# PEER encoder trunk on one core: the second half of each layer without GpSimd splits, one-hot products or gate rows

## Chip, core and metric

One core of a Trainium2 chip runs the whole program in one launch. The metric is device time in microseconds (us), median of several runs. The engines are named as the profile names them: PE (TensorE matmuls), PEld (its weight loads), DVE (VectorE), ACT (ScalarE), POOL (GpSimd), SP (SyncE, which issues the DMAs).

## What is computed

A bidirectional encoder trunk with `DEPTH` 2, `SEQ` 256, `D_MODEL` 1024. Each layer is a mixer (five head groups between an input and an output projection) followed by a PEER feed-forward, and the change lies in the second:

```python
def peer_ffn(xn, wq, subkeys, u_tab, v_tab):
    q = (xn @ wq).reshape(b, s, PEER_HEADS, 2, PEER_HALF)              # 8 heads, 2 x 128
    sc = jnp.einsum('bshjc,hjkc->bshjk', q, subkeys)                   # 128 keys per half
    top_s, top_i = lax.top_k(sc, PEER_TOPK)                            # 16 of 128, twice
    cand = top_s[..., 0, :, None] + top_s[..., 1, None, :]             # 16 x 16 sums
    best, ci = lax.top_k(cand, PEER_TOPK)
    i1 = take(top_i[..., 0, :], ci // 16); i2 = take(top_i[..., 1, :], ci % 16)
    g = jax.nn.softmax(best)
    # per token: experts idx = i1 * 128 + i2, 8 x 16 of 16384
    act = gelu(u_tab[idx] . x);  y = sum((g * act) * v_tab[idx])
```

## The kernel before

The kernel does not gather experts. It multiplies all 16,384 rows of `u` with all 256 tokens, writes gelu of that into a table `H` of 128 partitions x (128 blocks x 256 tokens), multiplies `H` by a gate that is zero for experts a token did not choose, and multiplies the product with all of `v`.

**Weights.** Every weight comes as a block of 128 x 1024 fp32 numbers (`w_raw`) through `Stream` (lines 56 to 97). For precision each block is split into a rounded part and a rest: `w_hi` is a cast on ACT (L82), `w_lo` a subtraction (L84) on DVE, or on POOL where the block's flag in `sources` says so. The two parts have three buffers each (pool `hl`), so a block can be split when PE has finished the third block before it. Every product is three matmuls (L238 to L240: `w_hi` with `xh`, `w_hi` with `xl`, `w_lo` with `xh`). The flag comes from `queue(aps, pool_every)` (L144): from the fifth query block on every fourth block goes to POOL (L152 to L154).

**Order of the PEER phase** (`peer_phase`, L807 on). Eight pairs of query blocks (L969), then 64 pairs of `u` blocks (L974), then 128 `v` blocks (L981). A pair is 48 matmuls of 256 columns into `ps_mm`. Beside the pairs runs the routing of the tokens, in two tiles of 128 tokens, as a generator `routing_steps`: `score_steps` (scores, then 16 of 128 by max, index, replace, max, index: L808 to L812), `best_steps` (sums of candidates on POOL, L821; 16 of the 50 candidate pairs, L835 to L839; then the chosen pair's number as a one-hot row of 50 (L849), its product with the candidates' expert numbers on POOL (L851), and the sum over the row (L857)). Each `yield` names a cost, and after each half pair `bg.advance(budget)` lets the generator go on for `B_Q` or `B_R`. It must be done when `u` reaches block `U_FREE` (L976), since its tables lie in the second half of `H`.

**Gates.** After the routing each `u` pair is followed by one step `gate_step` for 8 tokens (32 steps): `a2`, a one-hot of `i2` (DVE, L892); `a1`, a one-hot of `i1` in bf16 (DVE, L895); `ag` = `a1` times the gate (POOL, L897); eight matmuls (L907) give each token's 128 x 128 gate; DVE multiplies it into the blocks of `H` that are done (L912), ACT copies it into the others (L911). Blocks that come later are multiplied on DVE as they are made (L932).

Program order is not the order on the engines: the framework's scheduler reorders by priority and its own model of durations. On each engine instructions then run strictly in the order that it wrote.

Of the kernel before, what the change touches and what calls it, by code (L numbers as in the profile page):

```python
# [12 lines left out]
BF16 = mybir.dt.bfloat16  # L13
# [3 lines left out]
ALU = mybir.AluOpType  # L17
# [3 lines left out]
P = 128  # L21
T = 256
D = 1024
NC = D // P
NK = 128
# [6 lines left out]
MEM_CHUNK = 2  # L32
FIRST = {0: 1, 1: 2}
B_Q = 1.3
B_R = 1.7
U_FREE = 64
W_IN_PAIRS = {"pool": 0, "conv_a": 2, "gate": 4, "diff_q": 6, "diff_k": 8, "diff_v": 10,
              "sc_h": 12, "sc_bg": 14, "sc_cg": 16, "mem_q": 18}
# [5 lines left out]
NPAIR = sum(PAIR_LEN)  # L44
# [92 lines left out]
def build(tc, x, mem, w_in, w_kv, w_out, wq, u_t, v_t, subk, pool_w, conv_pw, vec, dist, inv_count, ind, out, depth=2,  # L137
          dbg=None):
    nc = tc.nc
    V, A, G = nc.vector, nc.scalar, nc.gpsimd  # L140
# [3 lines left out]
    def queue(aps, pool_every=0):  # L144
        sources.extend((ap, pool_every > 0 and n % pool_every == pool_every - 1) for n, ap in enumerate(aps))

    for l in range(depth):
        queue([w_kv[l, b] for b in range(4)])
        queue([w_in[l, W_IN_PAIRS[n] + c] for n in MIX["pairs"] for c in range(2)], MIX["pool_every"])
        queue([w_out[l, 2 * g + c] for g in MIX["groups"] for c in range(2)], 3)  # L150
        queue([wq[l, b] for b in range(4)])
        queue([wq[l, b] for b in range(4, 16)], 4)  # L152
        queue([u_t[l, i] for i in range(NK)], 4)
        queue([v_t[l, i] for i in range(NK)], 4)  # L154

    with (
        tc.tile_pool(name="const", bufs=1) as cp,
# [16 lines left out]

        ind_t = cp.tile([P, 3, P], F32, name="ind_t")
        ones_m, ind64, ind32 = ind_t[:, 0, :], ind_t[:, 1, :], ind_t[:, 2, :]
        iota_t = cp.tile([P, NK, 8], BF16, name="iota_t")
        G.iota(iota_t, pattern=[[1, NK], [0, 8]], base=0, channel_multiplier=0, allow_small_or_imprecise_dtypes=True)
        iota_i = cp.tile([P, NK], BF16, name="iota_i")
        V.tensor_copy(iota_i, iota_t[:, :, 0])  # L180
        iota_f = cp.tile([P, NK], F32, name="iota_f")
        V.tensor_copy(iota_f, iota_t[:, :, 0])
        mhalf = cp.tile([P, 1], F32, name="mhalf")
        V.memset(mhalf, -0.5)
        warm = cp.tile([P, 1], F32, name="warm")
# [551 lines left out]
        def peer_phase(l, pp, pb):  # L737
# [8 lines left out]
            def pt(shape, name, bufs=1, dt=F32, tag=None):  # L746
                return pp.tile(shape, dt, name=name, bufs=bufs, tag=tag or name)
# [7 lines left out]
            def carve(n, dt=F32):  # L755
                nonlocal o
                s = hf[:, o:o + n]
                o += n
                assert o <= NK * T
                return s if dt is F32 else s.bitcast(dt)  # L760
# [5 lines left out]
            sk = carve(2048).rearrange("p (a k) -> p a k", a=16)  # L766
            nc.sync.dma_start(sk, subk[l])

            i1T = pt([P, T], "i1T", dt=BF16)
            i2T = pt([P, T], "i2T")  # L770
            gT = pt([P, T], "gT")

            work = [carve(128) for _ in range(2)]
            oh = [carve(8 * NPAIR, BF16).rearrange("p (k n) -> p k n", k=16) for _ in range(2)]
            pr = [carve(16 * NPAIR).rearrange("p (k n) -> p k n", k=16) for _ in range(2)]
            tabs = []
            for tt in range(2):
# [15 lines left out]
            def score_steps(tt):  # L793

                tb = tabs[tt]
                for hq in range(4):
                    while done["q"] < 2 * hq + 2:
                        yield None
                    ps = acc_tile(hq, [P, 4, NK], "ps_sc")
                    for r in range(4):  # L800
                        hj = 4 * hq + r
                        nc.tensor.matmul(ps[:, r, :], qT[:, hj // 2, hj % 2, tt * P:(tt + 1) * P], sk[:, hj, :],
                                         start=True, stop=True)
                    for r in range(4):
                        hj = 4 * hq + r
                        h, j = hj // 2, hj % 2
                        m0, m1 = tb["top_s"][:, h, j, 0:8], tb["top_s"][:, h, j, 8:16]  # L807
                        V.max(m0, ps[:, r, :])  # L808
                        V.max_index(tb["top_i"][:, h, j, 0:8], m0, ps[:, r, :])
                        V.match_replace(work[tt], m0, ps[:, r, :], -3e38)  # L810
                        V.max(m1, work[tt])
                        V.max_index(tb["top_i"][:, h, j, 8:16], m1, work[tt])  # L812
                        yield 1.8
                top_s, top_f = tb["top_s"], tb["top_f"]
                V.tensor_copy(top_f, tb["top_i"])
                V.tensor_scalar(top_f[:, :, 0, :], top_f[:, :, 0, :], 128.0, None, op0=ALU.mult)
                for dst, src in ((tb["cand"], top_s), (tb["ecand"], top_f)):
                    for a in range(9):
                        n, off = PAIR_LEN[a], PAIR_OFF[a]
                        if a < 8:  # L820
                            G.tensor_add(dst[:, :, off:off + n], src[:, :, 1, 0:n],  # L821
                                         src[:, :, 0, a:a + 1].to_broadcast([P, 8, n]))
                        else:
                            G.tensor_add(dst[:, :, off:off + 8], src[:, :, 0, 8:16],
                                         src[:, :, 1, 0:1].to_broadcast([P, 8, 8]))
                yield 0.6

            def best_steps(tt):

                tb = tabs[tt]  # L830
                best, bi, cand, ecand = tb["best"], tb["bi"], tb["cand"], tb["ecand"]
                wk = work[tt][:, :NPAIR]
                for h in range(8):
                    m0, m1 = best[:, h, 0:8], best[:, h, 8:16]
                    V.max(m0, cand[:, h, :])  # L835
                    V.max_index(bi[:, h, 0:8], m0, cand[:, h, :])
                    V.match_replace(wk, m0, cand[:, h, :], -3e38)
                    V.max(m1, wk)
                    V.max_index(bi[:, h, 8:16], m1, wk)  # L839
                    yield 1.3  # L840
                fin, gs = tb["fin"], tb["gs"]
                gx = fin[:, 2, :].rearrange("p (h k) -> p h k", h=8)
                V.tensor_sub(gx, best, best[:, :, 0:1].to_broadcast([P, 8, 16]))
                A.activation(gx, gx, AF.Exp)
                V.tensor_copy(tb["bib"], bi)
                yield 0.6

                def one_hot(h):
                    V.tensor_tensor(out=oh[h % 2], in0=iota_i[:, None, :NPAIR].to_broadcast([P, 16, NPAIR]),  # L849
                                    in1=tb["bib"][:, h, :, None].to_broadcast([P, 16, NPAIR]), op=ALU.is_equal)  # L850
                    G.tensor_mul(pr[h % 2], oh[h % 2], ecand[:, h, None, :].to_broadcast([P, 16, NPAIR]))  # L851

                one_hot(0)
                for h in range(8):
                    if h < 7:
                        one_hot(h + 1)
                    V.tensor_reduce(tb["es"][:, h, :], pr[h % 2], axis=AX.X, op=ALU.add)  # L857
                    yield 2.0
                ei = tb["ei"]
                V.tensor_copy(ei[:, 0, :], tb["es"].rearrange("p h k -> p (h k)"))  # L860
                V.tensor_scalar(ei[:, 1, :], ei[:, 0, :], 7, None, op0=ALU.arith_shift_right)
                V.tensor_scalar(ei[:, 2, :], ei[:, 0, :], 127, None, op0=ALU.bitwise_and)
                V.tensor_copy(fin[:, 0:2, :], ei[:, 1:3, :])
                yield 1.0
                V.tensor_reduce(gs, gx, axis=AX.X, op=ALU.add)
                V.reciprocal(gs, gs)
                V.tensor_mul(gx, gx, gs[:, :, None].to_broadcast([P, 8, 16]))
                yield 0.8
                ps = psum([P, 3, P], "ps_rt")
                for i in range(3):  # L870
                    nc.tensor.transpose(ps[:, i, :], fin[:, i, :], ident)
                s = slice(tt * P, (tt + 1) * P)
                A.copy(i1T[:, s], ps[:, 0, :])
                A.copy(i2T[:, s], ps[:, 1, :])
                A.copy(gT[:, s], ps[:, 2, :])
                yield 0.0
# [8 lines left out]
            GT = 8  # L885
            one_hots = {}

            def gate_one_hots(g):

                s = slice(GT * g, GT * g + GT)  # L890
                a2 = pt([P, GT, NK], "a2", bufs=2)
                V.tensor_tensor(out=a2, in0=iota_f[:, None, :].to_broadcast([P, GT, NK]),  # L892
                                in1=i2T[:, s, None].to_broadcast([P, GT, NK]), op=ALU.is_equal)
                a1 = pt([P, NK, GT], "a1", dt=BF16)
                V.tensor_tensor(out=a1, in0=iota_t, in1=i1T[:, None, s].to_broadcast([P, NK, GT]), op=ALU.is_equal)  # L895
                ag = pt([P, GT, NK], "ag", bufs=2)
                G.tensor_mul(ag, a1.rearrange("p i t -> p t i"), gT[:, s, None].to_broadcast([P, GT, NK]))  # L897
                one_hots[g] = (a2, ag)

            def gate_group(g):  # L900
# [176 lines left out]
```

## Time and profile before

| | |
|---|---|
| Median of 3 runs | 2061.68 us (2061.6 to 2062.93) |
| The profiled execution | 2062.52 us, of which its span 2060.7 us |
| PE busy | 1981.6 us (96%) |
| DVE busy | 1477.6 us (72%) |
| ACT, POOL busy | 984.4 us (48%), 769.5 us (37%) |
| `w_lo` on DVE, on POOL | 468 and 144 of them, mean 1.350 and 2.579 us |
| `ag` on POOL (L897) | 64, mean 3.016 us |
| Chain that ended last | PE 70%, DVE 21%, issue 3%, POOL 3% |
| DMA | 331.48 MB, mean 161 GB/s |

The two layers follow each other, 1021 us apart. In layer 0 the PEER phase's matmuls begin near 173 us, the routing lies between 188 and 384 us, the gates end near 666 us, and the `v` blocks run from 684 us to beyond 1030 us, into the next mixer. A share of the whole span says little here; each of these stretches has its own limit.

### The profile page before, as it was taken

To read this page: it belongs to the slowest core of one execution; us is meant where nothing else is said; L and a number is where in the kernel's file an instruction comes from. 1 tells how busy PE (TensorE), PEld (TensorE's weight loads), DVE (VectorE), ACT (ScalarE), POOL (GpSimd) and SP (SyncE) were. 2 spreads that over 40 slices of the span, in tenths; PEclk is the share of its full clock that TensorE was granted. 3 is DMA by queue.
4 is the path that set the end of the run, shared out by engine and by line. 5 is a ranking of instruction groups with operands and counts; after the bars stand their busy time and mean duration, and the time that the engine had idled before them with its cause. 6 is when DMAs were issued, how large, how long until landed. Compare 5 with 4: busy or idle time off the path is not lost.

```text
span 2060.7 us, 33441 instructions
## 1 busy us (share of the span) xinstructions
PE 1981.6 (96%) x13122; PEld 1818.7 (88%) x13122; DVE 1477.6 (72%) x2195; ACT 984.4 (48%) x1474; POOL 769.5 (37%) x430
## 2 busy tenths in 40 slices
PE   8899989899999999999999999889999999999999
PEld 7878988899999888888898789889999998888887
DVE  6875799669999554454478668995799995445454
ACT  7664444344433544444466644344444334444443
POOL 3721346435555222222236213572455541221221
PEclk9999999999999999999999999999999999999999
DMA  6324444444434655555553244435444345555554
GB/s 215 117 76 169 166 144 144 164 164 143 134 134 139 205 192 190 194 190 192 191 169 114 87 168 166 144 133 177 151 144 144 123 143 194 192 187 196 192 188 160
DMA packets 92766, 331.48 MB, mean 161 GB/s; under 512 B 10816, under 2 KB 11712, under 8 KB 92352
## 3 DMA queue, kind: packets, MB, share of 16 engines
q1 hardware_dynamic: 92608, 329.34, 47.0%
q8 instruction: 103, 1.69, 0.3%
q14 instruction: 55, 0.45, 0.1%
HBM read 328.25 MB, written 1.05 MB: 160 GB/s over the span
## 4 chain that ended last, share of the span: by engine, by line
PE 70%; DVE 21%; issue 3%; POOL 3%; ACT 2%; DMA 1%; SPq 0%; DVEq 0%; POOLq 0%; ACTq 0%
PE acc_v L268 11%; PE acc_v L271 11%; PE acc_v L267 11%; PE ps_mm L240 9%; PE ps_mm L238 9%; PE ps_mm L239 9%; DVE w_lo L84 6%; PE ps_g L907 4%; DVE H L849 2%; DVE H L857 1%; DVE a L892 1%; POOL cv_ac L436 1%; DVE H L932 1%; DVE a L895 1%; ACT w_hi L82 1%
## 5 line engine op out<-in xcount | busy, mean ns | idle before, releaser
L82 ACT CAST w_hi<-w_raw 128x1024 fp32r<-128x1024 f32 x612 | 641.4, 1049 | 790.1 <-PE ps_mm L239 445.5
L84 DVE TENSOR_TENSOR w_lo<-w_raw,w_hi 128x1024 fp32r<-128x1024 f32 x468 | 629.8, 1350 | 248.1 <-ACT w_hi L82 248.0
L240 PE MATMUL ps_mm<-xh,w_lo 128*128 128x256 f32 x2624 | 753.3, 288 | 39.0 <-DVE w_lo L84 36.8
L238 PE MATMUL ps_mm<-xh,w_hi 128*128 128x256 f32 x2624 | 754.5, 289 | 1.2 <-ACT H L934 1.2
L239 PE MATMUL ps_mm<-xl,w_hi 128*128 128x256 f32 x2624 | 749.5, 286 | 0.0
L84 POOL TENSOR_TENSOR w_lo<-w_raw,w_hi 128x1024 fp32r<-128x1024 f32 x144 | 371.3, 2579 | 892.4 <-ACT w_hi L82 872.5
L240 PEld LDWEIGHTS ps_mm<-xh,w_lo 128*128 128x128 f32 x2624 | 508.1, 194 | 46.2 <-DVE w_lo L84 43.4
L238 PEld LDWEIGHTS ps_mm<-xh,w_hi 128*128 128x128 f32 x2624 | 507.2, 194 | 3.1 <-ACT H L934 1.6
L239 PEld LDWEIGHTS ps_mm<-xl,w_hi 128*128 128x128 f32 x2624 | 508.7, 194 | 0.9 <-DVE xl L229 0.5
L268 PE MATMUL acc_v<-w_lo,a_hi 128*128 128x512 f32 x1016 | 316.5, 392 | 0.0
L271 PE MATMUL acc_v<-w_hi,a_lo 128*128 128x512 f32 x1016 | 315.4, 392 | 0.0
L947 DVE TENSOR_TENSOR a_lo<-H,a_hi 128x512 fp32r<-128x512 f32 x128 | 120.4, 942 | 239.1 <-ACT a_hi L945 239.0
L267 PE MATMUL acc_v<-w_hi,a_hi 128*128 128x512 f32 x1016 | 274.0, 391 | 0.0
L897 POOL TENSOR_TENSOR ag<-a,gT 128x1024 f32<-128x1024 bf16 x64 | 193.0, 3016 | 183.6 <-PE ps_g L907 104.1
L271 PEld LDWEIGHTS acc_v<-w_hi,a_lo 128*128 128x128 f32 x1016 | 190.9, 188 | 42.3
L267 PEld LDWEIGHTS acc_v<-w_hi,a_hi 128*128 128x128 f32 x1016 | 190.9, 188 | 41.6
L268 PEld LDWEIGHTS acc_v<-w_lo,a_hi 128*128 128x128 f32 x1016 | 191.1, 188 | 40.6
L945 ACT CAST a_hi<-H 128x512 fp32r<-128x512 f32 x128 | 79.4, 622 | 154.8 <-PE acc_v L268 149.6
L932 DVE TENSOR_TENSOR H<-tmp,H 128x16 f32<-128x16 f32 (+16 forms) x68 | 152.0, 2236 | 0.0
L907 PE MATMUL ps_g<-ag,a 128*128 128x128 f32 x1024 | 126.0, 275 | 1.3 <-POOL ag L897 1.3
L907 PEld LDWEIGHTS ps_g<-ag,a 128*128 128x128 f32 x1024 | 120.5, 192 | 1.7 <-POOL ag L897 1.7
L892 DVE TENSOR_TENSOR a<-iota_f,i2T 128x1024 f32<-128x1024 f32 x64 | 85.4, 1337 | 6.7 <-PE ps_g L907 6.7
(244 smaller groups left out, 1607.1 us busy)
## 6 DMA issues: line engine op xcount, KB each, us to landing
w_raw<-u_t SPq DMA_DIRECT2D x256, 512.0 KB, 3.3
w_raw<-v_t SPq DMA_DIRECT2D x256, 512.0 KB, 4.2
w_raw<-w_in SPq DMA_DIRECT2D x40, 512.0 KB, 3.5
w_raw<-wq SPq DMA_DIRECT2D x32, 512.0 KB, 3.3
w_raw<-w_out SPq DMA_DIRECT2D x20, 512.0 KB, 3.2
w_raw<-w_kv SPq DMA_DIRECT2D x8, 512.0 KB, 4.3
H<-subk SPq DMA_DIRECT2D x2, 1024.0 KB, 4.8
mem_t<-mem SPq DMA_DIRECT2D x4, 256.0 KB, 6.4
```

The lines of the kernel that those rows point to most:

```text
L82: self.nc.scalar.copy(hi, r)
L84: (self.nc.gpsimd if on_pool else self.nc.vector).tensor_sub(lo, r, hi.bitcast(F32))
L238: nc.tensor.matmul(ps, wh, xh[:, c, :], start=(c == 0), stop=False)
L239: nc.tensor.matmul(ps, wh, xl[:, c, :], start=False, stop=False)
L240: nc.tensor.matmul(ps, wl, xh[:, c, :], start=False, stop=(c == NC - 1))
L267: nc.tensor.matmul(accs[tt][hf], ah[:, s], hi[:, n], start=start, stop=False)
L268: nc.tensor.matmul(accs[tt][hf], ah[:, s], lo[:, n], start=False, stop=False)
L271: nc.tensor.matmul(accs[tt][hf], al[:, s], hi[:, n], start=False, stop=False)
L897: G.tensor_mul(ag, a1.rearrange("p i t -> p t i"), gT[:, s, None].to_broadcast([P, GT, NK]))
L907: nc.tensor.matmul(ps[:, t, :], a2[:, 4 * q + t, :], ag[:, 4 * q + t, :], start=True, stop=True)
L932: V.tensor_mul(sl[:, :, :g], tmp[:, :, :g], sl[:, :, :g])
L947: V.tensor_sub(al, src, ah.bitcast(F32))
```

## The change

From the query weights on no block is flagged for POOL, so DVE splits them all. The product L851 moves from POOL to DVE, and its one-hot row is laid out with the 16 chosen ranks innermost, compared against a table `iota_i` of 50 x 16. `a1` and its table `iota_t` go away: `ag` is made by eight DVE instructions of 128 elements, one for each token, that compare with `i1` and multiply by the gate at once, both given per partition; `i1T` is fp32 for that. POOL keeps the sums of candidates (L821, L824) there. `B_R` and the costs in the yields are others, so the generator is cut differently. The mixer's flags stay.

```diff
-B_R = 1.7
+B_R = 1.4
...
-        queue([wq[l, b] for b in range(4)])
-        queue([wq[l, b] for b in range(4, 16)], 4)
-        queue([u_t[l, i] for i in range(NK)], 4)
-        queue([v_t[l, i] for i in range(NK)], 4)
+        queue([wq[l, b] for b in range(16)])
+        queue([u_t[l, i] for i in range(NK)])
+        queue([v_t[l, i] for i in range(NK)])
...
-        iota_t = cp.tile([P, NK, 8], BF16, name="iota_t")
-        G.iota(iota_t, pattern=[[1, NK], [0, 8]], base=0, channel_multiplier=0, allow_small_or_imprecise_dtypes=True)
-        iota_i = cp.tile([P, NK], BF16, name="iota_i")
-        V.tensor_copy(iota_i, iota_t[:, :, 0])
+        iota_i = cp.tile([P, NPAIR, 16], BF16, name="iota_i")
+        G.iota(iota_i, pattern=[[1, NPAIR], [0, 16]], base=0, channel_multiplier=0, allow_small_or_imprecise_dtypes=True)
         iota_f = cp.tile([P, NK], F32, name="iota_f")
-        V.tensor_copy(iota_f, iota_t[:, :, 0])
+        G.iota(iota_f, pattern=[[1, NK]], base=0, channel_multiplier=0, allow_small_or_imprecise_dtypes=True)
...
-            i1T = pt([P, T], "i1T", dt=BF16)
+            i1T = pt([P, T], "i1T")
...
-            oh = [carve(8 * NPAIR, BF16).rearrange("p (k n) -> p k n", k=16) for _ in range(2)]
+            oh = [carve(8 * NPAIR, BF16).rearrange("p (n k) -> p n k", k=16) for _ in range(2)]
...
-                        yield 1.8
+                        yield 1.2
...
-                    yield 1.3
+                    yield 0.8
...
                 def one_hot(h):
-                    V.tensor_tensor(out=oh[h % 2], in0=iota_i[:, None, :NPAIR].to_broadcast([P, 16, NPAIR]),
-                                    in1=tb["bib"][:, h, :, None].to_broadcast([P, 16, NPAIR]), op=ALU.is_equal)
-                    G.tensor_mul(pr[h % 2], oh[h % 2], ecand[:, h, None, :].to_broadcast([P, 16, NPAIR]))
-
-                one_hot(0)
+                    V.tensor_tensor(out=oh[h % 2], in0=iota_i, in1=tb["bib"][:, h, None, :].to_broadcast([P, NPAIR, 16]),
+                                    op=ALU.is_equal)
+                    V.tensor_mul(pr[h % 2], oh[h % 2].rearrange("p n k -> p k n"),
+                                 ecand[:, h, None, :].to_broadcast([P, 16, NPAIR]))
+
                 for h in range(8):
-                    if h < 7:
-                        one_hot(h + 1)
+                    one_hot(h)
                     V.tensor_reduce(tb["es"][:, h, :], pr[h % 2], axis=AX.X, op=ALU.add)
-                    yield 2.0
+                    yield 2.4
...
-                a1 = pt([P, NK, GT], "a1", dt=BF16)
-                V.tensor_tensor(out=a1, in0=iota_t, in1=i1T[:, None, s].to_broadcast([P, NK, GT]), op=ALU.is_equal)
                 ag = pt([P, GT, NK], "ag", bufs=2)
-                G.tensor_mul(ag, a1.rearrange("p i t -> p t i"), gT[:, s, None].to_broadcast([P, GT, NK]))
+                for t in range(GT):
+                    k = GT * g + t
+                    V.tensor_scalar(ag[:, t, :], iota_f, i1T[:, k:k + 1], gT[:, k:k + 1], op0=ALU.is_equal, op1=ALU.mult)
```

Three places show how the order on the engines moves. Line numbers of the changed kernel are three lower through the routing and four lower from L857 on; `H<-H` is routing work, whose tables lie in `H`.

DVE, two gate steps of layer 0 before the change:

```order
L932 TENSOR_TENSOR H<-tmp,H 128x2x24
L892 TENSOR_TENSOR a_5034<-iota_f,i2T 128x1024
L912 TENSOR_TENSOR H<-ps_g,H 128x66x4 x2
L895 TENSOR_TENSOR a_5121<-iota_t,i1T 128x1024
L84 TENSOR_TENSOR w_lo<-w_raw,w_hi 128x1024 x2
L932 TENSOR_TENSOR H<-tmp,H 128x2x32
L892 TENSOR_TENSOR a_5119<-iota_f,i2T 128x1024
L912 TENSOR_TENSOR H<-ps_g,H 128x68x4 x2
L895 TENSOR_TENSOR a_5206<-iota_t,i1T 128x1024
L84 TENSOR_TENSOR w_lo<-w_raw,w_hi 128x1024
```

The same engine and place in the changed kernel:

```order
L928 TENSOR_TENSOR H<-tmp,H 128x2x24
L888 TENSOR_TENSOR a_4995<-iota_f,i2T 128x1024
L908 TENSOR_TENSOR H<-ps_g,H 128x64x4
L893 TENSOR_SCALAR ag<-iota_f,i1T,gT 128x128 x5
L908 TENSOR_TENSOR H<-ps_g,H 128x64x4
L893 TENSOR_SCALAR ag<-iota_f,i1T,gT 128x128 x3
L84 TENSOR_TENSOR w_lo<-w_raw,w_hi 128x1024 x2
```

A step now has two splits always, and eight short instructions in place of the compare L895.

DVE, one-hot rows of the first token tile in the changed kernel (a compare L846, a product L848, a sum L853 for each head):

```order
L84 TENSOR_TENSOR w_lo<-w_raw,w_hi 128x1024
L853 TENSOR_REDUCE H<-H 128x16
L846 TENSOR_TENSOR H<-iota_i,H 128x800
L853 TENSOR_REDUCE H<-H 128x16
L846 TENSOR_TENSOR H<-iota_i,H 128x800
L808 MAX H<-H 128x8
L84 TENSOR_TENSOR w_lo<-w_raw,w_hi 128x1024
L848 TENSOR_TENSOR H<-H 128x800
L84 TENSOR_TENSOR w_lo<-w_raw,w_hi 128x1024
L848 TENSOR_TENSOR H<-H 128x800
```

Before, L851 stood in POOL's order and DVE had L849 and L857 alone; heads now come in twos, with three splits between one pair of sums and the next.

POOL, from the last sums of candidates of layer 0 on, before the change:

```order
L824 TENSOR_TENSOR H<-H 128x8x8
L84 TENSOR_TENSOR w_lo<-w_raw,w_hi 128x1024
L897 TENSOR_TENSOR ag<-a_4690,gT 128x1024
L84 TENSOR_TENSOR w_lo<-w_raw,w_hi 128x1024
L897 TENSOR_TENSOR ag<-a_4696,gT 128x1024
L851 TENSOR_TENSOR H<-H 128x800 x4
```

and in the changed kernel:

```order
L818 TENSOR_TENSOR H<-H 128x8x2 x3
L821 TENSOR_TENSOR H<-H 128x8x8
L195 MEMSET mm_kz 128x1024
L195 MEMSET mm_vz 128x1024
L195 MEMSET pw 128x256
```

After the sums POOL has nothing until the next layer's mixer.

## Rows read from the trace of the kernel before

**Rows 1.** Stretches: us, busy (count) of PE PEld DVE ACT POOL, clock, DMA

```profile
260.00:400.00 140.00, 123.96 (x987) 121.49 (x986) 127.23 (x264) 55.82 (x67) 77.89 (x47) 0.96 0.43 147
600.00:690.00 90.00, 86.55 (x699) 84.58 (x698) 80.98 (x73) 37.84 (x71) 42.15 (x14) 1.00 0.45 153
720.00:1000.00 280.00, 280.00 (x1225) 229.94 (x1224) 139.45 (x127) 133.90 (x154) 62.73 (x26) 1.00 0.57 191
1281.00:1421.00 140.00, 123.74 (x985) 121.00 (x984) 127.27 (x262) 55.63 (x67) 78.25 (x47) 0.98 0.43 147
```

**Rows 2.** What PE waited for, whole span: us in total, times, longest

```profile
PE ps_mm L240 <- DVE w_lo L84: 36.8, 30, 3.2
```

**Rows 3.** PE in order of time, one gate step: start us, us, instruction

```profile
501.51 1.95 PE L907 MATMUL ps_g<-ag,a 128*128 128x128 f32 x16
...
503.41 0.28 PE L239 MATMUL ps_mm<-xl,w_hi 128*128 128x256 f32 x1
...
509.05 1.95 PE L907 MATMUL ps_g<-ag,a 128*128 128x128 f32 x16
510.75 0.36 PE L238 MATMUL ps_mm<-xh,w_hi 128*128 128x256 f32 x1
```

**Rows 4.** The first stretch, `ps_mm` matmuls alone: PE busy (count), clock

```profile
260.00:400.00 140.00, 119.33 (x934) 0.96 0.43 147
```

**Rows 5.** The gate step on DVE, then POOL, in order of time

```profile
500.60 0.68 DVE L895 TENSOR_TENSOR a<-iota_t,i1T 128x1024 bf16<-128x1024 bf16 x1
...
503.85 2.49 DVE L932 TENSOR_TENSOR H<-tmp,H 128x160 f32<-128x160 f32 x1
...
507.80 0.48 DVE L912 TENSOR_TENSOR H<-ps_g,H 128x320 f32<-128x320 f32 x1
...
503.54 2.63 POOL L897 TENSOR_TENSOR ag<-a,gT 128x1024 f32<-128x1024 bf16 x1 [4.94 <-PE ps_g L907]
507.37 2.76 POOL L84 TENSOR_TENSOR w_lo<-w_raw,w_hi 128x1024 fp32r<-128x1024 f32 x1 [1.21 <-ACT w_hi L82]
```

**Rows 6.** DVE by line and form, L932: busy us, mean ns, idle before

```profile
L932 DVE TENSOR_TENSOR H<-tmp,H 128x272 f32<-128x272 f32 x2 | 5.2, 2618 | 0.0
...
L932 DVE TENSOR_TENSOR H<-tmp,H 128x288 f32<-128x288 f32 x2 | 0.9, 446 | 0.0
...
L932 DVE TENSOR_TENSOR H<-tmp,H 128x16 f32<-128x16 f32 x2 | 0.3, 162 | 0.0
```

**Rows 7.** DVE in order of time, routing stretch

```profile
226.44 0.29 DVE L808 MAX8 H<-ps_sc 128x8 f32<-128x128 f32 x1
...
227.37 1.21 DVE L84 TENSOR_TENSOR w_lo<-w_raw,w_hi 128x1024 fp32r<-128x1024 f32 x1
228.49 0.09 DVE L810 MATCH_VALUE_LOAD H<-H,ps_sc 128x8 f32 x1
...
228.76 0.29 DVE L808 MAX8 H<-ps_sc 128x8 f32<-128x128 f32 x1
...
229.89 0.28 DVE L810 MATCH_REPLACE8 H<-H,ps_sc 128x128 f32<-128x128 f32 x1
230.20 0.30 DVE L811 MAX8 H<-H 128x8 f32<-128x128 f32 x1
...
247.23 0.87 DVE L835 MAX8 H<-H 128x8 f32<-128x50 f32 x7
...
283.55 0.96 DVE L857 TENSOR_REDUCE H<-H 128x16 f32<-128x800 f32 x1
284.44 0.97 DVE L849 TENSOR_TENSOR H<-iota_i,H 128x800 bf16<-128x800 bf16 x1
```

**Rows 8.** DVE with a scalar per partition: count, ns min/median/max, starts, form

```profile
L215 DVE TENSOR_SCALAR rn_ms<-rn_ss x8: 203/207/215, 16.8 to 1191.2; 128x1 f32<-128x1 f32 x8
...
L218 DVE TENSOR_SCALAR H<-xt,rn_rs x4: 475/482/486, 169.3 to 1192.1; 128x512 f32<-128x512 f32 x4
```

**Rows 9.** A DVE copy that reads bf16 at steps of 16 bytes, same columns

```profile
L180 DVE COPY iota_i<-iota_t x1: 261/261/261, 3.4 to 3.4; 128x128 bf16<-128x128 bf16 x1
```

## The prediction

> **What bounds the kernel now.** I read the busy time by stretches first, then PE's waits, then single instructions in order of time. Over the whole span PE looks full, so a gain can only come from stretches where it is not. In the `v` blocks it has no hole: 280.00 of 280 us [rows 1]. In 260 to 400 us, where the tokens are routed, it has 123.96 of 140, while DVE has 127.23; near the end of the gates (600 to 690) it has 86.55 of 90. Layer 1 repeats this 1021 us later. So 16.0 and 3.45 us a layer are PE's idle time. The waits name who ended it: PE's matmuls with `w_lo` waited 36.8 us for DVE's splits [rows 2], nearly all of twice 19.5. This is the whole field for the change, with what the clock adds.
>
> That part is found by counting matmuls. Between 503.41 and 509.05 lie 47 starts of `ps_mm`, 0.120 us each; the 16 passes of a gate burst take 1.70, 0.106 each; a whole gate step, 501.51 to 509.05, takes 7.54 [rows 3]. In 260 to 400 us PE did 934 `ps_mm` [rows 4] and 53 others: 934 x 0.120 + 53 x 0.106 = 117.7 us. It lost 22.3 of 140: 16.0 idle, 6.3 at the lower granted clock (mean 0.96 there) and in restarting. A layer thus loses 22.3 + 3.45 = 25.75 us, both 51.5.
>
> DVE's busy time is partly waiting. L932 on 160 elements took 2.49 us, and ended 0.17 after POOL's `ag`, which ran from 503.54 to 506.17; L912, which reads one side from PSUM, took 0.48 inside a POOL split [rows 5]. By form it is plainer: 288 elements took 0.446 us where POOL was free, 272 took 2.618 where it was not [rows 6]. A DVE instruction with two SBUF inputs waits here for POOL's to end.
>
> **The change, part by part.** Durations overlap: a split of 1.21 is followed 1.12 later by the next instruction [rows 7]. I use start to start, 0.08 less than a duration. From 16 and 288 elements [rows 6], an fp32 instruction costs 0.145 + 1.04 ns an element.
>
> *Gate steps.* Gone are the compare L895 and the POOL product with the waits that it caused. Added are half a split and eight `ag` instructions. One scalar per partition and one element take 0.207, 512 elements 0.482 [rows 8]: 0.54 ns an element, so 128 take 0.276, 0.195 start to start. No row has two scalars. If the second costs as much as the first (0.207 against 0.145), it is 0.255; at 1.04 ns an element it would be 0.32. Ends 0.195 and 0.32; I take 0.23, between the first two, since the rows with 512 elements are the nearest. The last step, the dearest: two splits 2.26, `a2` (a split's form) 1.13, eight `ag` 1.84, L912 twice on 4 x 120 and L932 on 2 x 240 elements, 1.69: 6.92 us under PE's 7.54. At 0.32 it is 7.64, which passes PE only in the last steps. So the 3.45 us go, twice: **6.9 us**.
>
> *Routing stretch.* The changed order on DVE is dense from the phase's 21st to its 64th weight block. Between those splits it holds: 44 splits, 49.7 us; 91 score instructions at 0.205 to 0.275 (five take 1.20, 226.44 to 228.76 less the split [rows 7]), 22.3; 80 on 50 elements (seven take 0.87 [rows 7], 0.115 each, 0.175 to 0.185 with a value load), 12.4; 16 products at 0.90, as the old compare of 800 elements (0.97), 14.4; 15 sums at 0.89, 13.4; 16 compares, whose inputs now both run contiguously in bf16 as L895's do, which took 0.68 for 1024 [rows 5], so 0.48, 7.7; four `a2` and 32 `ag`, 11.9; small ones 3.8. Sum 135.6 us. PE's own time for these blocks: 44 x 24 x 0.120 = 126.7, and 6.8 for scores, transposes and the two first gate groups: 133.5. So DVE is just over PE. To it come waits for its own results: L811 starts 0.31 after L810 where it needs it, 0.20 where something stands between [rows 7], so 0.11 each; bounds none and all 91 + 80, 19 us; I take 40 of them, 4.5, because the scheduler mixes two chains. From it goes a lead of about 3 (two blocks of 2.88, less cast and split). 135.6 + 4.5 - 133.5 - 3 = 3.6. The order is uneven: the first gate rows put 7.3 us between two splits, and the four blocks of the first one-hot heads hold 15.5 where PE needs 11.5. I add 2.5 for these two: 6 us idle, and 2 at the lower clock, by the ratio of today (6.3 to 16.0). Eight of 22.3 stay, 14.3 go, twice: **28.6 us**. Ends: 2 stay (no own waits, no clock), 40.6 won; 17 stay (most own waits exposed), 10.6 won.
>
> The product is the one new form in it, since it reads the one-hot row at steps of 32 bytes. A copy of 128 bf16 elements at steps of 16 bytes took 0.261 [rows 9], 0.91 ns an element over 0.145, no slower than an fp32 element; hence 0.90. The Trainium skill (SBUF — State Buffer, section on the DMA port swizzle, note on cachelines) says that SBUF has 16-byte lines and that an access to a new line each time pays a penalty, without an amount. This row shows none at 16 bytes; at 32 none is shown. By that rule the sum would be the first rival's.
>
> *At nothing.* In the `v` blocks DVE takes the fourth split, 1.13 in 11 us, of which it is busy half (139.45 of 280); the cover is that half, and without it a split would delay PE by its 1.13. The candidates' sums stay on POOL, and a DVE cast may still wait for one; that lies inside the ends above. Tables at the start are made while the first weights load. Mixer order is unchanged up to the query weights. No DMA changes; a raw buffer is freed by DVE in 1.2 us [rows 7] instead of by POOL in 2.8 [rows 5].
>
> **Sum.** The profiled execution took 2062.52 us (span 2060.7, 1.8 around it); the median of the runs is 0.84 lower. 2062.5 - 6.9 - 28.6 = 2027.0; against the median I say **2026 us**.
>
> **The rivals.**
> 1. *The product's stride costs.* At half as much or double per element, 16 products add 6.6 to 13.3 us a layer to a stretch where DVE is just over PE; with the clock's share 8 to 16. Time 2042 to 2058. For it: no row reads at 32 bytes. Against: the copy at 16. Chance 0.10.
> 2. *DVE stays the bound of the routing.* Own waits are hardly covered, since the new order has long runs of one chain (compare, product, sum of the same head), and 17 to 22 of 22.3 stay. Time 2045 to 2055. For it: DVE's sum is already level with PE's. Against: its waits behind POOL are gone. Chance 0.12.
> 3. *Slower: gate rows bound DVE.* A step is 4.08 + 0.033 j + 8 a, with a the start to start of one `ag` and j from 0 to 29. It passes 7.54 at the last step from a = 0.31 on. It eats the 17.75 us won in a layer when the sum of the excess over 30 steps reaches that: 0.1 x 30 + 14.5 at a = 0.445; from there the change loses. At 0.50 the excess is 30.7, 13 more than won, twice: 2088 us. For it: 256 instructions a layer of a form that no row has. Against: the rows with one scalar, which are half that. Chance 0.06.
> 4. *The wait was not POOL's.* If L932 keeps its 2.2 us without POOL, a gate step is 1 us over PE: 2 x (32 - 14.3) = 35 us slower, 2097. Against it stand both forms in one kernel [rows 6]. Chance 0.02.
>
> **How the numbers follow.** The forecast has 0.70, with its own range 2015 to 2045 from the ends above (2062.5 - 6.9 - 40.6 and - 10.6). The whole field is 51.5 us, so nothing lies under 2010. The range goes to 2012 at the low end, for a lead that I made too small, and to 2050 at the other, over most of rivals 1 and 2; outside stay rivals 3 and 4 and the tails, under 0.2. A measurement here tells about 0.2% from no change, 4.1 us, so faster means under 2057.6: 0.70 + 0.10 + 0.12 less their upper tails, 0.88. Same: 0.04. Slower: 0.08.
>
> **What would show it.** POOL has no split and no `ag` from the query weights on. L932's forms lie on one line, 0.16 to 0.69 us, with no step of 2.2. PE has no idle time in 600 to 690, and less than half of 16 in the routing. `ag` takes 0.27 to 0.34 us, the new compare near 0.56, the product near 0.97. I am wrong if PE still waits over 12 us a layer for `w_lo`, if the product takes 1.4 or more, or if DVE is full through the gate steps.

## The result and the profile after

The changed kernel took **2036.33 us** (median of 4 runs, 2035.27 to 2037.62) against 2062.01 of the kernel before: ratio 0.9875, 95% interval 0.9858 to 0.9892. The forecast was 2026, its range 2012 to 2050. So 26 us were won where 35.5 were forecast. The profiled execution spans 2033.5 us, 27.2 less than before.

The stretches of [rows 1] (first to third lines: routing, end of the gates, `v` blocks; fourth: the routing of layer 1):

```profile
260.00:400.00 140.00, 131.90 (x1062) 129.19 (x1061) 132.68 (x298) 60.91 (x73) 6.38 (x18) 0.99 0.47 158
600.00:690.00 90.00, 90.00 (x678) 86.31 (x678) 69.08 (x111) 42.37 (x73) 0.00 (x0) 1.00 0.51 171
720.00:1000.00 280.00, 280.00 (x1225) 229.94 (x1224) 160.38 (x153) 133.79 (x154) 0.00 (x0) 1.00 0.55 191
1281.00:1421.00 140.00, 130.07 (x1052) 126.75 (x1051) 124.09 (x245) 57.72 (x69) 6.37 (x18) 1.00 0.47 162
```

PE's idle time at the end of the gates is gone. In the routing it fell from 16.0 to 8.1 us in layer 0 and from 16.3 to 9.9 in layer 1. POOL is nearly empty. PE's wait for the splits, to be laid beside [rows 2]:

```profile
PE ps_mm L237 <- DVE w_lo L84: 16.5, 19, 1.5
```

Where the gain lies is read from two landmarks in each layer: the start of the second norm (L218 before [rows 8], L215 now) and the start of the last `ps_mm` matmul. First these matmuls before the change, layer 0, then layer 1 (count, ns, starts):

```profile
L240 PE MATMUL ps_mm<-xh,w_lo x1312: 275/283/583, 28.7 to 683.3; 128*128 128x256 f32 x188
L240 PE MATMUL ps_mm<-xh,w_lo x1312: 277/283/470, 1051.0 to 1704.3; 128*128 128x256 f32 x188
L218 DVE TENSOR_SCALAR H<-xt,rn_rs x2: 479/482/486, 169.3 to 171.5; 128x512 f32<-128x512 f32 x2
L218 DVE TENSOR_SCALAR H<-xt,rn_rs x2: 475/480/486, 1189.9 to 1192.1; 128x512 f32<-128x512 f32 x2
```

The same rows of the changed kernel:

```profile
L237 PE MATMUL ps_mm<-xh,w_lo x1312: 278/283/469, 29.3 to 669.2; 128*128 128x256 f32 x188
L237 PE MATMUL ps_mm<-xh,w_lo x1312: 278/283/470, 1036.9 to 1677.0; 128*128 128x256 f32 x188
L215 DVE TENSOR_SCALAR H<-xt,rn_rs x2: 476/481/486, 169.7 to 171.9; 128x512 f32<-128x512 f32 x2
L215 DVE TENSOR_SCALAR H<-xt,rn_rs x2: 478/482/485, 1175.7 to 1177.9; 128x512 f32<-128x512 f32 x2
```

From landmark to landmark: 514.0 and 514.4 us before, 499.5 and 501.3 now. That is 14.5 + 13.1 = 27.6 us, the whole difference of the spans (27.2) and 0.4 more; the mixer and the `v` blocks together gave nothing. Less the 3.45 us of the gates, the routing gave 11.0 and 9.7 us a layer where 14.3 were forecast.

The instructions that the change touches, on DVE (count, ns min/median/max, starts, form): the product, the compare, `ag`; then L928 (L932 before) by form, with busy us and mean ns, to be laid beside [rows 6]:

```profile
L848 DVE TENSOR_TENSOR H<-H x32: 1649/1694/1746, 270.6 to 1389.3; 128x800 f32<-128x800 bf16 x32
L846 DVE TENSOR_TENSOR H<-iota_i,H x32: 551/562/582, 267.9 to 1381.8; 128x800 bf16<-128x800 bf16 x32
L893 DVE TENSOR_SCALAR ag<-iota_f,i1T,gT x512: 325/342/394, 354.1 to 1644.1; 128x128 f32<-128x128 f32 x171
...
L928 DVE TENSOR_TENSOR H<-tmp,H 128x288 f32<-128x288 f32 x2 | 0.9, 452 | 0.0
L928 DVE TENSOR_TENSOR H<-tmp,H 128x272 f32<-128x272 f32 x2 | 0.9, 435 | 0.0
...
L928 DVE TENSOR_TENSOR H<-tmp,H 128x16 f32<-128x16 f32 x2 | 0.3, 170 | 0.0
```

272 elements, which took 2618 ns before, take 435. The compare is as forecast (0.56), `ag` at the upper edge. The **product takes 1.694 us where 0.97 was forecast**: (1.694 - 0.145) / 800 = 1.94 ns an element in place of 1.04. Sixteen of them cost a layer 16 x 0.72 = 11.6 us more of DVE than the forecast had. In order of time two products, 3.30 us, stand ahead of the next split and of the next reduction (first head pairs of layer 0):

```profile
270.63 3.30 DVE L848 TENSOR_TENSOR H<-H 128x800 f32<-128x800 bf16 x2
...
274.23 1.22 DVE L84 TENSOR_TENSOR w_lo<-w_raw,w_hi 128x1024 fp32r<-128x1024 f32 x1
...
275.73 0.95 DVE L853 TENSOR_REDUCE H<-H 128x16 f32<-128x800 f32 x1
276.58 0.58 DVE L846 TENSOR_TENSOR H<-iota_i,H 128x800 bf16<-128x800 bf16 x1
```

### The profile page after: what moved, and what is told of

It is laid out like the page before. It is cut to its first block, busy times and chain, and to the rows that moved or that the text cites. A ratio compares the mean times of both kernels' runs of the same rounds, so it can differ in the third digit from the quotient of the medians.

```text
span 2033.5 us, 33742 instructions
## 1 busy us (share of the span) xinstructions
PE 1973.2 (97%) x13122; PEld 1811.5 (89%) x13122; DVE 1494.1 (73%) x2809; ACT 985.4 (48%) x1474; POOL 165.0 (8%) x201
## 3 DMA queue, kind: packets, MB, share of 16 engines
q8 instruction: 103, 1.69, 0.3%
HBM read 328.25 MB, written 1.05 MB: 162 GB/s over the span
## 4 chain that ended last, share of the span: by engine, by line
PE 82%; DVE 10%; ACT 3%; issue 3%; POOL 3%; DMA 1%; SPq 0%; DVEq 0%; POOLq 0%; ACTq 0%
PE ps_mm L237 13%; PE ps_mm L235 13%; PE ps_mm L236 13%; PE acc_v L265 11%; PE acc_v L268 11%; PE acc_v L264 11%; PE ps_g L903 5%; DVE w_lo L84 3%; DVE H L848 2%; POOL cv_ac L433 1%; ACT w_hi L82 1%; DVE ag L893 1%; DVE H L853 1%; PE ps_sc L799 1%; PE acc_o L264 1%
## 5 line engine op out<-in xcount | busy, mean ns | idle before, releaser
L84 DVE TENSOR_TENSOR w_lo<-w_raw,w_hi 128x1024 fp32r<-128x1024 f32 x602 | 743.0, 1235 | 394.6 <-ACT w_hi L82 392.6
L237 PE MATMUL ps_mm<-xh,w_lo 128*128 128x256 f32 x2624 | 748.3, 286 | 16.8 <-DVE w_lo L84 16.5
L943 DVE TENSOR_TENSOR a_lo<-H,a_hi 128x512 fp32r<-128x512 f32 x128 | 88.5, 693 | 77.5 <-ACT a_hi L941 77.5
L893 DVE TENSOR_SCALAR ag<-iota_f,i1T,gT 128x128 f32<-128x128 f32 x512 | 142.0, 343 | 0.0
L888 DVE TENSOR_TENSOR a<-iota_f,i2T 128x1024 f32<-128x1024 f32 x64 | 77.8, 1218 | 0.0
L908 DVE TENSOR_TENSOR H<-ps_g,H 128x240 f32<-128x240 f32 (+31 forms) x128 | 66.2, 523 | 0.1
```

Source lines behind the costliest of these rows:

```text
L84: (self.nc.gpsimd if on_pool else self.nc.vector).tensor_sub(lo, r, hi.bitcast(F32))
L237: nc.tensor.matmul(ps, wl, xh[:, c, :], start=False, stop=(c == NC - 1))
L893: V.tensor_scalar(ag[:, t, :], iota_f, i1T[:, k:k + 1], gT[:, k:k + 1], op0=ALU.is_equal, op1=ALU.mult)
L943: V.tensor_sub(al, src, ah.bitcast(F32))
```

## The experiments

The theory was that the product's access at 32-byte steps is the cause of the smaller gain, and that the splits and gate rows on POOL were what held DVE before. "After" is the changed kernel. Medians are of 4 runs each (E9 one), beside 2063.67 (E1, E2, E3, E5), 2063.78 (E4, E6, E7, E8) and 2062.78 us (E10) of the kernel before on the same chips. Idle is PE's in 260 to 400 and in 1281 to 1421 us; the last column is what PE waited for DVE's `w_lo` in all.

| | edit | us | ratio (95%) | PE idle | w_lo |
|---|---|---|---|---|---|
| | before | 2062.0 | 1 | 16.0, 16.3 | 36.8 |
| | after | 2036.3 | 0.9875 (0.9858 to 0.9892) | 8.1, 9.9 | 16.5 |
| E1 | after, one-hot row laid out as before | 2022.8 | 0.9802 (0.9785 to 0.9818) | 5.9, 5.7 | 5.8 |
| E2 | after, wide steps on the written side | 2033.0 | 0.985 (0.9834 to 0.9867) | 8.6, 8.7 | 16.3 |
| E8 | after, 16-byte steps | 2033.8 | 0.9857 (0.9841 to 0.9874) | 8.6, 9.3 | 17.5 |
| E6 | after, old costs in the yields | 2034.9 | 0.9861 (0.9845 to 0.9878) | 7.6, 8.5 | 12.4 |
| E7 | E1, old costs in the yields | 2023.6 | 0.9805 (0.9788 to 0.9821) | 5.3, 4.7 | 4.2 |
| E3 | before, gate rows changed | 2045.4 | 0.9912 (0.9895 to 0.9929) | 13.8, 13.0 | 27.5 |
| E4 | before, all splits on DVE | 2032.2 | 0.9845 (0.9829 to 0.9862) | 8.1, 7.2 | 13.5 |
| E5 | before, splits and gate rows | 2030.4 | 0.9839 (0.9823 to 0.9856) | 6.2, 6.4 | 6.7 |
| E10 | before, product on DVE | 2052.8 | 0.9948 (0.9931 to 0.9965) | 12.7, 11.0 | 26.0 |

**E1: the layout undone.** The compare and the product run as in the kernel before, with 50 innermost, but on DVE:

```diff
-  V.tensor_tensor(out=oh[h % 2], in0=iota_i, in1=tb["bib"][:, h, None, :].to_broadcast([P, NPAIR, 16]), op=ALU.is_equal)
-  V.tensor_mul(pr[h % 2], oh[h % 2].rearrange("p n k -> p k n"), ecand[:, h, None, :].to_broadcast([P, 16, NPAIR]))
+  V.tensor_tensor(out=oh[h % 2], in0=iota_i[:, None, :].to_broadcast([P, 16, NPAIR]),
+                  in1=tb["bib"][:, h, :, None].to_broadcast([P, 16, NPAIR]), op=ALU.is_equal)
+  V.tensor_mul(pr[h % 2], oh[h % 2], ecand[:, h, None, :].to_broadcast([P, 16, NPAIR]))
```

> The changed kernel with the one-hot row laid out as before (50 innermost), so that the product on VectorE reads it contiguously and the compare is the old one. Theory (the product's 1.69 us come from reading at 32-byte steps): product 0.97, compare 0.97 instead of 0.56, VectorE 0.31 us less for each of 16 heads a layer, 5 us a layer in a stretch where it is full; time 2022 to 2030 us. Rival (the 1.69 come from mixing bf16 with fp32 or from the broadcast): product stays 1.69, compare 0.97, VectorE 6.5 us a layer more; time 2044 to 2052.

2022.78 us (2022.17 to 2023.8), 13.5 less than after. Its product and compare, the stretches of the routing, and PE's waits:

```profile
L848 DVE TENSOR_TENSOR H<-H x32: 980/985/993, 271.5 to 1384.0; 128x800 f32<-128x800 bf16 x32
L846 DVE TENSOR_TENSOR H<-iota_i,H x32: 974/984/992, 267.9 to 1380.0; 128x800 bf16<-128x800 bf16 x32
...
260.00:400.00 140.00, 134.11 (x1110) 132.90 (x1110) 130.86 (x300) 63.71 (x76) 6.42 (x18) 1.00 0.52 166
1281.00:1421.00 140.00, 134.31 (x1112) 133.10 (x1111) 120.52 (x242) 62.38 (x81) 6.42 (x18) 1.00 0.54 172
...
PE ps_mm L235 <- ACT H L929: 7.6, 4, 2.2
PE ps_mm L237 <- DVE w_lo L84: 5.8, 9, 1.5
```

Its landmarks:

```profile
L237 PE MATMUL ps_mm<-xh,w_lo x1312: 277/283/469, 28.1 to 663.4; 128*128 128x256 f32 x188
L237 PE MATMUL ps_mm<-xh,w_lo x1312: 277/283/469, 1031.1 to 1663.9; 128*128 128x256 f32 x188
L215 DVE TENSOR_SCALAR H<-xt,rn_rs x2: 477/482/486, 168.7 to 170.9; 128x512 f32<-128x512 f32 x2
L215 DVE TENSOR_SCALAR H<-xt,rn_rs x2: 477/482/487, 1169.9 to 1172.1; 128x512 f32<-128x512 f32 x2
```

The change's layout makes the compare 0.422 us faster and the product 0.709 slower: 16 x 0.287 = 4.6 us a layer lost on DVE. From landmark to landmark E1 takes 494.7 and 494.0 us, 4.8 and 7.3 less than after. So DVE's time in the routing still passes on to PE, in full in layer 0; why layer 1 gains more than 4.6 is open. With E7, which is level with it, this is the fastest version here; ACT's gelu (L929) is now the larger wait.

**E2: wide steps on the written side.** The product reads the row contiguously and writes fp32 at steps of 200 bytes:

```diff
-  V.tensor_mul(pr[h % 2], oh[h % 2].rearrange("p n k -> p k n"), ecand[:, h, None, :].to_broadcast([P, 16, NPAIR]))
+  V.tensor_mul(pr[h % 2].rearrange("p k n -> p n k"), oh[h % 2], ecand[:, h, :, None].to_broadcast([P, NPAIR, 16]))
```

> The changed kernel with the product walked in the one-hot row's own order: it reads the row contiguously and writes fp32 results at steps of 200 bytes. Theory (reads at wide steps cost, and writes do not): product 0.97, compare 0.56, VectorE 11.6 us less a layer; time 2015 to 2024 us. If wide steps cost on either side: product 1.69, time 2036 as the changed kernel. Rival (mixed types): 1.69 and 2036 as well, so this run tells only together with the contiguous one.

2032.99 us (2030.68 to 2035.43), with the product at:

```profile
L848 DVE TENSOR_TENSOR H<-H x32: 1621/1664/1702, 271.0 to 1387.1; 128x800 f32<-128x800 bf16 x32
```

So the 2015 to 2024 us of the theory did not come: here steps of 200 bytes in the write cost about as much as steps of 32 in the read. As E1's product, of the same types, took 0.985, the mixed types are not the cause.

**E8: steps of 16 bytes.** The one-hot row stands as two groups of eight ranks, so that the product reads it at the step that [rows 9] has:

```diff
-  oh = [carve(8 * NPAIR, BF16).rearrange("p (n k) -> p n k", k=16) for _ in range(2)]
+  oh = [carve(8 * NPAIR, BF16).rearrange("p (a n k) -> p a n k", a=2, k=8) for _ in range(2)]
```

> The changed kernel with the 16 ranks of a one-hot row laid out as two groups of 8, so that the product reads it at steps of 16 bytes instead of 32; the compare still runs contiguously. Theory (16-byte steps run at one element a cycle, as the copy in the trace of before did, and only wider ones cost): product 0.97 to 1.0, compare 0.56, VectorE 11.7 us a layer less than the changed kernel and 6.7 less than the contiguous one; 2013 to 2021 us. Rival (each access that leaves its 16-byte line costs a second cycle): product 1.69, 2036 us.

2033.8 us (2032.09 to 2035.49):

```profile
L849 DVE TENSOR_TENSOR H<-H x32: 1551/1622/1669, 270.4 to 1387.1; 128x800 f32<-128x800 bf16 x32
```

Against the theory, the product pays at 16 bytes nearly all that it pays at 32. So it was not the distance between the row's 16 bytes and the change's 32 that misled the forecast, but the reading of [rows 9] itself. E9 asks that.

**E9: a probe.** E1 with sixteen DVE instructions of 192 elements at the start of layer 0's PEER phase, which read a bf16 table at four steps (once shown, run twice):

```diff
+  V.tensor_copy(po, pv[:, 0:192])
+  V.tensor_copy(po, pv[:, 0:768:4])
+  V.tensor_copy(po, pv[:, 0:1536:8])
+  V.tensor_copy(po, pv[:, 0:3072:16])
+  V.tensor_mul(pf2, pv[:, 0:192].rearrange("p (a k) -> p a k", a=3), two)
...
```

> E1's kernel plus a probe on VectorE at the start of layer 0's PEER phase, sixteen instructions of 192 elements on a bf16 table: a copy to bf16 and a product with an fp32 row to fp32, each reading the table contiguously and at steps of 8, 16 and 32 bytes, twice. Theory (an element in a 16-byte line of its own costs one more cycle, about 0.9 ns, whatever the instruction, and a copy's contiguous pace is about half of a product's): copy 0.25 us or less contiguously and at 8 bytes, near 0.32 at 16 and 32 bytes; product near 0.35 contiguously and at 8 bytes, near 0.51 at 16 and 32. Rival (only instructions with two inputs pay, so that row 9 was right for copies): the four copies alike within 0.03 us. Third way (steps cost in proportion to their size): 8, 16 and 32 bytes all differ. The whole kernel: within 3 us of E1, 2023 to 2026.

Copies at 2, 8, 16 and 32 bytes (L796 to L799), then products (L800 to L803):

```profile
L796 DVE COPY H<-H x2: 199/200/201, 174.7 to 177.4; 128x192 bf16<-128x192 bf16 x2
L797 DVE COPY H<-H x2: 253/253/253, 175.1 to 177.8; 128x192 bf16<-128x192 bf16 x2
L798 DVE COPY H<-H x2: 321/326/332, 176.1 to 178.6; 128x192 bf16<-128x192 bf16 x2
L799 DVE COPY H<-H x2: 327/328/330, 176.7 to 179.6; 128x192 bf16<-128x192 bf16 x2
L800 DVE TENSOR_TENSOR H<-H,iota_f x2: 351/356/360, 174.8 to 177.5; 128x192 f32<-128x192 bf16 x2
L801 DVE TENSOR_TENSOR H<-H,iota_f x2: 351/351/351, 175.3 to 177.9; 128x192 f32<-128x192 bf16 x2
L802 DVE TENSOR_TENSOR H<-H,iota_f x2: 491/495/499, 176.3 to 178.8; 128x192 f32<-128x192 bf16 x2
L803 DVE TENSOR_TENSOR H<-H,iota_f x2: 494/497/500, 177.0 to 179.9; 128x192 f32<-128x192 bf16 x2
```

Over a start of 0.145 us (that of the fp32 products in [rows 6]; a copy's own was not measured), a copied element costs 0.29 ns contiguously, 0.94 at 16 bytes and 0.95 at 32; an element of the product 1.10, 1.82 and 1.83. At 8 bytes the product pays nothing, the copy part. [Rows 9] has 0.91 ns: that copy was already paying, by this reckoning three times its contiguous price, and looked cheap only because it was held against another instruction's 1.04. The Trainium skill (SBUF — State Buffer, section on the DMA port swizzle, note on cachelines) wants at least two accesses to a 16-byte line; the jump between 8 and 16 bytes agrees with it, and the copy's rise at 8 bytes is not given by it. The one run took 2029.38 us, more than the 2023 to 2026 expected: the memset ahead of the probe (2.62 us) delays the norm and its transposes, and where the rest went is open.

**E6 and E7: the costs.** The change with the costs of before, and E1 with them:

```diff
-B_R = 1.4
+B_R = 1.7
...
-                        yield 1.2
+                        yield 1.8
...
-                    yield 0.8
+                    yield 1.3
...
-                    yield 2.4
+                    yield 2.0
```

> The changed kernel with B_R 1.7 and the old costs in the generator. Theory (what matters is VectorE's work, not how the generator is cut): 2030 to 2042 us, idle time of TensorE in the routing 6 to 11 us a layer. Rival (the new cut brings a good part of the gain): 2046 or more.

> The contiguous layout (2022.8 us) with B_R 1.7 and the old costs in the generator. Theory (VectorE's work decides): 2018 to 2028 us. Rival (the cut decides): 2033 or more.

2034.85 us (2031.42 to 2035.07) and 2023.57 (2022.45 to 2026.13). In both pairs the intervals of the ratio overlap: the new cut of the generator is worth nothing that can be told here.

**E3: gate rows alone.** The kernel before with `ag` made as in the change, all else as it was.

> The kernel before with the gate rows fused per token and nothing else; GpSimd keeps every fourth split and the product. Theory (a VectorE instruction with two SBUF inputs waits for GpSimd's to end): the H multiply waits only in steps with a GpSimd split, TensorE's 3.45 us of idle time near the end of the gates go, the routing keeps most of its 16; 2046 to 2056 us. Rival (the wait was not GpSimd's): the H multiply keeps about 2.5 us, eight short instructions replace one compare, VectorE passes TensorE in each step; over 2066.

2045.42 us (2044.65 to 2047.29), just under the range of the theory:

```profile
260.00:400.00 140.00, 126.24 (x1018) 124.36 (x1017) 131.22 (x294) 57.93 (x69) 68.74 (x44) 0.98 0.47 150
600.00:690.00 90.00, 90.00 (x704) 87.45 (x704) 73.18 (x121) 40.47 (x72) 14.80 (x6) 1.00 0.52 162
```

The idle time at the end of the gates is gone, and the routing, where the first gate rows and POOL's share of the splits lie, is 2.3 us better (3.3 in layer 1).

**E4: splits alone.** The kernel before with one edit, product and `ag` still on POOL:

```diff
-        queue([wq[l, b] for b in range(4)])
-        queue([wq[l, b] for b in range(4, 16)], 4)
-        queue([u_t[l, i] for i in range(NK)], 4)
-        queue([v_t[l, i] for i in range(NK)], 4)
+        queue([wq[l, b] for b in range(16)])
+        queue([u_t[l, i] for i in range(NK)])
+        queue([v_t[l, i] for i in range(NK)])
```

> The kernel before with all splits from the query weights on given to VectorE and nothing else; GpSimd keeps the one-hot product and the gate product. Theory (half a split more in a step is paid, while the H multiply waits 2.2 us behind the gate product as before): VectorE over TensorE in the late gate steps, idle time in 600 to 690 us 5 to 12 a layer instead of 3.45; in the routing less, 9 to 13 instead of 16; 2052 to 2072 us. Rival (the splits on GpSimd were the main cost): 2045 or less.

2032.18 us (2030.44 to 2034.24), far below what the theory expected, and no slower than the whole change: the rival, that the splits on POOL were the main cost, holds. The theory had DVE wait behind `ag` in every gate step and PE with it. DVE does wait, as its order of time shows in a late step (with POOL's `ag` last):

```profile
636.55 1.21 DVE L891 TENSOR_TENSOR a<-iota_f,i2T 128x1024 f32<-128x1024 f32 x1
...
638.84 4.53 DVE L84 TENSOR_TENSOR w_lo<-w_raw,w_hi 128x1024 fp32r<-128x1024 f32 x2
643.28 0.63 DVE L931 TENSOR_TENSOR H<-tmp,H 128x464 f32<-128x464 f32 x1
...
644.39 1.21 DVE L891 TENSOR_TENSOR a<-iota_f,i2T 128x1024 f32<-128x1024 f32 x1
...
639.56 2.72 POOL L896 TENSOR_TENSOR ag<-a,gT 128x1024 f32<-128x1024 bf16 x1 [5.10 <-PE ps_g L906]
```

The two splits take 4.53 us beside `ag`; the next two, beside an idle POOL, take 2.35 (646.09). Yet the step, from one L891 to the next, takes 7.84, the longest of the last ones, and PE's gate bursts follow each other every 7.54 us to the end. In the kernel before, two late steps on DVE look like this:

```profile
641.91 1.21 DVE L892 TENSOR_TENSOR a<-iota_f,i2T 128x1024 f32<-128x1024 f32 x1
...
644.18 4.51 DVE L84 TENSOR_TENSOR w_lo<-w_raw,w_hi 128x1024 fp32r<-128x1024 f32 x2
648.62 2.79 DVE L932 TENSOR_TENSOR H<-tmp,H 128x448 f32<-128x448 f32 x1
...
651.89 1.21 DVE L892 TENSOR_TENSOR a<-iota_f,i2T 128x1024 f32<-128x1024 f32 x1
...
658.64 1.21 DVE L892 TENSOR_TENSOR a<-iota_f,i2T 128x1024 f32<-128x1024 f32 x1
```

The first waits twice, behind `ag` and then behind a split on POOL, and takes 9.98 us; the next waits once and takes 6.75. Together that is 16.73 where PE needs 15.08. One wait in each step nearly fits, and its small excess at the end does not reach PE; a second wait in every other step does.

**E5: splits and gate rows, product still on POOL.**

> The kernel before with two parts of the change: all splits on VectorE and the gate rows fused per token; the product stays on GpSimd with the old layout, and the costs in the generator are the old ones. Theory (the gain is the waits behind GpSimd that go, and the product on VectorE gives part of it back): TensorE idle near the end of the gates 0 instead of 3.45 us a layer, in the routing 5 to 10 instead of 16; 2022 to 2036 us, at or under the changed kernel. Rival (the gain comes from the new cut of the generator): 2045 or more.

2030.44 us (2028.91 to 2031.67). Against E4 the intervals overlap: once the splits are off POOL, the gate rows bring little more. Against the whole change they do not (0.9858 to 0.9892 there), nor against E1 (0.9785 to 0.9818): moving the product to DVE cost time with the change's layout and won some with the contiguous one.

**E10: product alone.** The kernel before with `V.tensor_mul(pr...)` in place of `G.tensor_mul(pr...)`, the row laid out contiguously:

> The kernel before with one edit: the product runs on VectorE instead of GpSimd, with the one-hot row laid out as before, so that it reads contiguously. Splits and gate rows stay as before. Theory (with the splits still on GpSimd, VectorE bounds the routing and still waits behind them; the product adds 16 x 0.90 = 14.4 us a layer to it and takes away only what the compares waited, 16 x 0.17): no gain, 2060 to 2085, with the product at 1.0 us where GpSimd is free and longer beside a split. Rival (the sixteen products on GpSimd, 2.4 us each, delay VectorE by more than they cost on it): 2050 or less.

2052.77 us (2051.67 to 2053.68), between the two: DVE wins back from POOL more than the theory allowed, less than the rival asked. Most of PE's wait for the splits stays:

```profile
PE ps_mm L240 <- DVE w_lo L84: 26.0, 23, 3.1
PE ps_mm L240 <- POOL w_lo L84: 7.2, 2, 3.6
```

**The parts together.** Alone, each against the median of the kernel before that stands beside it, the splits gave 31.6 us, the gate rows 18.3, the product with the old layout 10.0. That is 59.9, more than the prediction's whole field of 51.5; all three give 40.2 (E7, which like the change also makes each head's row only just before its sum). So they empty in part the same idle time. The layout takes back 11 to 14 us (E6 against E7, after against E1).

## Why the prediction came out as it did

- **What bounds the kernel** held. PE's waits for `w_lo` fell from 36.8 to 16.5 us, and the gain lies between the two landmarks of each layer alone.
- **DVE waits behind POOL** held: L928's forms lie on one line. That such a wait always costs time did not: E4 keeps one in each gate step, and PE loses nothing there.
- **Gate steps, 6.9 us**: held, 90.00 of 90 us. `ag` takes 0.342 us at the median; five in a row take 1.36, so (1.36 - 0.34) / 4 = 0.255 start to start, within the ends 0.195 and 0.32 and above the 0.23 taken:

```profile
635.28 1.36 DVE L893 TENSOR_SCALAR ag<-iota_f,i1T,gT 128x128 f32<-128x128 f32 x5
```

- **The product at 0.90: the step that failed.** It was priced from [rows 9] as "no slower than an fp32 element", with the sentence that the row shows no penalty at 16 bytes. Start to start it measured about 1.61 (1.69 less 0.08). E8 shows the penalty at 16 bytes, E9 shows it in a copy, so the row did hold it. The mechanism of rival 1 is what happened, with nearly double the price per element (1.94 against 1.04 ns).
- **The rest of the routing's sum was too dear**, and this hid part of the first error: that the time fell inside the range is partly luck, since two errors ran against each other. With the product at 1.694, rival 1 gave 2042 to 2058; 2036 was measured. The trace of the changed kernel shows which terms. This is the stretch that the prediction added up, from the split of the phase's 21st weight block to that of the 65th, in layer 0 and in layer 1:

```profile
233.40:384.10 150.70, 143.33 (x1161) 140.82 (x1161) 149.39 (x421) 65.80 (x78) 12.74 (x36) 0.99 0.45 155
1240.00:1391.80 151.80, 142.60 (x1161) 139.49 (x1160) 149.16 (x420) 65.98 (x78) 12.72 (x36) 1.00 0.45 153
```

  It holds the 44 splits, 16 products, 16 compares, 15 sums and 32 `ag` of the forecast. With the product at 1.62 and `ag` at 0.256 from start to start, the forecast's 135.6 us for DVE is 147.9. The stretch takes 150.7 and 151.8, so DVE's own waits cost 2.8 and 3.9, not 4.5. Of PE's 1161 matmuls 1094 are `ps_mm`; at the forecast's 0.120 and 0.106 they are 138.4 us of work, so the lead, and whatever else PE's 133.5 left out, was 4.9 and not 3. PE lost the difference, 12.3 and 13.4 us, where 22.3 were lost before: 7.4 and 9.2 idle, the rest in slower matmuls. So nothing came on top of DVE's time for unevenness (2.5) and the clock (2): what PE loses to them lies inside the time that it would have waited for DVE. E1 agrees. Its product costs what was forecast (0.985) and its compare 0.42 more, 6.8 us a layer, and still the routing gave more than the 14.3 forecast: 494.7 and 494.0 us from landmark to landmark are 19.3 and 20.4 less than before, 15.9 and 17.0 without the gates' 3.45.
- **Rivals 2, 3 and 4**: in the changed kernel DVE still bounds the routing, but 9.7 to 11.0 us a layer went, not the few of rival 2; `ag` stayed under 0.31; the waits were POOL's.
- **The cuts, the `v` blocks, the tables** at nothing: held (E6, E7; 280.00 of 280 us with DVE at 160.38).
- Of the signs named, "less than half of 16 us idle in the routing" just missed (8.1 and 9.9), and "the product takes 1.4 or more" came true.

## What to carry to other kernels

Price a stepped access by rows of the same instruction, contiguous and stepped; a stepped copy that looks no dearer than another kind of instruction may already pay a multiple of its own price. Where a one-hot row serves a compare and a product, reckon both layouts: here the compare won 0.42 us and the product lost 0.71. Where one engine bounds a stretch, what the other loses to its clock or to an uneven order lies inside that bound and is not added to it. And test a bundle's parts alone: one edit, the splits, did no worse than the bundle (0.9845 against 0.9875), since the stall that it left nearly fits under the engine that bounds the step, and since the bundle's stepped product cost more than it won.

## What the runs showed of the hardware that was not expected

- DVE's two-input product of 800 elements takes 0.985 us contiguously, 1.622 and 1.694 when it reads bf16 at 16 and 32 bytes, and 1.664 when it writes fp32 at 200 bytes: 1.85 to 1.94 ns an element, in place of 1.05.
- A bf16 copy costs, over a start of 0.145 us, 0.29 ns an element contiguously, 0.56 at 8 bytes, 0.94 at 16 (E9). The product pays nothing at 8 bytes, where two elements share 16 bytes.
- An instruction on DVE with two scalars per partition on 128 fp32 elements takes 0.342 us, 0.255 from start to start.
- A wait of DVE behind POOL of 2.2 us in each gate step of 7.54 us cost PE nothing (E4); with a second one in every other step DVE needs 16.73 us for two late steps.
